# Two-layer hybrid decoder trunk on one core: where Softplus is finished, and which engines do the last LayerNorm of the second token tile

## The chip, the cores and the metric

The kernel runs on one core of a Trainium2 chip. The core has a matrix engine (TensorE, PE in the profile, with its weight loads shown as PEld), a vector engine (VectorE, DVE), an activation engine (ScalarE, ACT), a general engine (GpSimd, POOL) and a queue engine that mostly starts DMAs (SyncE, SP). Each engine works through its own instructions in order. PE writes its products into PSUM, eight banks of 128 partitions by 512 floats; the other tiles lie in SBUF. The metric is the device time of one execution in microseconds (us); less is better.

## The reference

The input is x, 256 tokens by 2048 channels. Two layers are applied, and each ends in `x <- LayerNorm(alpha * x + mixer(x))` with alpha = 4^0.25.

- Layer 0 projects x to z, xs, B, C, dt, q, k, v and a gate. The columns xs, B and C go through a causal convolution with four taps and a SiLU. `dt = softplus(dt + dt_bias)` gives the step of a state-space scan (Mamba-2 SSD, one chunk of 256 positions), beside a causal attention with 16 heads. Both results are joined and projected back.
- Layer 1 is a diagonal complex state-space mixer (S5) between an input and an output projection, with a GLU.

```
dt = jax.nn.softplus(dt.astype(f32) + dt_bias.astype(f32))
a = -jnp.exp(a_log.astype(f32))
y = ssd_chunked_scan(xh * dt[..., None], dt * a, bm, cm)
...
y = (xf - mu) * lax.rsqrt(var + LN_EPS) * g.astype(jnp.float32) + b.astype(jnp.float32)
```

All matrix products are to be near float32 in precision.

## The kernel before

**Products.** Every large weight matrix is cut into units of 128 partitions by 1024 floats, 432 in all, in the order of use. For each unit `split_to` (L217) issues a load on SP (`raw`), an ACT copy that rounds it to the fast matmul type (`wh`, L239), and a DVE subtraction that leaves the remainder (`wl`, L244). A product is the sum of three terms (high by high, high by low, low by high). `raw`, `wh` and `wl` have four buffers each, and splits are issued three units ahead of the matmuls. The matmuls of the products stand at L288 (tokens on the partitions), L310, and L343 with L344 (channels on the partitions, `product_wide`). A product alternates between two pairs of PSUM banks. The last product keeps the split tiles of all its eight units, in the pool `tp2` (L1424).

**Small work between units.** Everything else is a job: a Python function that issues a few instructions. After each unit `pump` (L260) issues some jobs of the queue `jobs`, spread so that the queue is empty at the product's end, and some of the slower queue `back`. `run` (L254) asks that a job's instructions come behind the splits of the unit two ahead. The framework then orders each engine's instructions, near this program order.

**Softplus.** `dt_mm` (L491) multiplies x by the 32 dt columns. `dt_jobs` (L508) makes five jobs on 32 partitions by 256 tokens: `soft1` (ACT and DVE: exp and a reciprocal), `soft2` and `soft3` (GpSimd, L528 to L539: a polynomial of 19 instructions), `soft4` (L541: one step that ends Softplus, L545; a scan over positions, L550; the cumulated decay as high and low parts, L551 and L552) and `turn` (L554: four small PE transposes, L559 and L560, and two ACT copies into `dts` and `cums`). `dts`, `cums` and `cumhl` are read by the head jobs of the scan, which begin in a later product.

**The xs products.** The loop at L819 runs four `product_wide` products, j = 0 to 3, for 512 xs columns each. `xs_jobs` (L803) queues, after product j, the four convolution taps of j and their SiLU (L578, L583), the transposes of the columns j - 1 that were held back, and more by j: for j = 0 the four C·B products of `cb_job` (L596) and then `soft4` and `turn`; for j = 1 `trig_job` (L616), which also loads a table on SP. These jobs are issued during product j + 1. `soft1` to `soft3` are queued ahead, so they are issued during product 0.

**The end.** The last weight matrix has four products of 512 output columns; the loop at L1435 runs the first three. After each, `res1` (L1430) adds alpha times the old x into `x1` and takes the column statistics (L1433), for the token tiles t = 0 and 1. The fourth product is `product_apart` (L392): all its matmuls for tokens 0 to 127 (t = 0), then all for tokens 128 to 255 (t = 1). After each half `after1` (L1440) queues `first` (the last `res1`, the mean and variance at L1068, adding the epsilon at L1069, the root on ACT at L1070, the reciprocal at L1071, minus mean over deviation at L1444) and four pieces of columns. Piece 3 (320 columns) is one ACT instruction (L1451) and two on GpSimd (L1452, L1453); pieces 0 to 2 (576 columns each) are two DVE instructions each: subtract the mean and multiply by the gain (L1455), then multiply by the reciprocal and add the shift (L1456). A DMA per piece (L1457) stores the rows, on SP for pieces 1 and 3 and on ACT's queue for 0 and 2. The gain and shift rows are in `gb1`, loaded on POOL's queue (L1427, L1428).

Of the kernel before, what the change touches and what calls it, by code (L numbers as in the profile page):

```python
# [9 lines left out]
F32 = mybir.dt.float32  # L10
F32R = mybir.dt.float32r
AF = mybir.ActivationFunctionType
OP = mybir.AluOpType
PSUM = bass.MemoryType.PSUM
DRAM = bass.MemoryType.DRAM

P = 128
S = 256
# [5 lines left out]
HU = KT // HK  # L24
ALPHA = 4.0 ** 0.25
NKEEP = 6
NFIRST = 4
WARM0 = 8
WARM1 = 14
# [2 lines left out]
EPS = 1e-5  # L32
# [137 lines left out]
def trunk(tc, io, out):  # L170
    nc = tc.nc
    V, A, G, T = nc.vector, nc.scalar, nc.gpsimd, nc.tensor
    count = [0]

    def nm(s):
        count[0] += 1
        return f"{s}_{count[0]}"

    with ExitStack() as top:
# [10 lines left out]
        def C(name):  # L190
            lo, hi = CONST[name]
            return ct[:, lo:hi]
# [5 lines left out]
        ident = C("ident")  # L198

        def aux():  # L200
            return auxp.tile([P, 512], F32, tag="aux", name=nm("aux"))

        def big(tag, shape, dt=F32):
            return slot.tile(shape, dt, tag=tag, name=nm(tag))
# [43 lines left out]
        jobs = deque()  # L248
# [21 lines left out]
        def drain():  # L270
            while jobs:
                run(jobs.popleft())
# [6 lines left out]
        def banks():  # L279
            turnno[0] += 1  # L280
            return [main.tile([P, 512], F32, tag=f"m{turnno[0] % 2}{o}", name=nm("main")) for o in range(2)]
# [110 lines left out]
        def product_apart(hl, nu, nk, after, mid=None):  # L392
            ps = banks()
            cap = unit[0] + nu + NFIRST - 1
            for u in range(nu - nk):
# [26 lines left out]
        def transpose4(dst, srcs):  # L422
            for i, s in enumerate(srcs):
                end = T.transpose(dst[:, i * P : i * P + P], s, ident)  # L424
            return end
# [17 lines left out]
        mr1 = cst.tile([P, 2, 4], F32, name="mr1")  # L443
        st0 = cst.tile([P, 2, 4, 6], F32, name="st0")
        st1 = cst.tile([P, 2, 4, 6], F32, name="st1")
# [4 lines left out]
        with ExitStack() as l0:  # L450
# [3 lines left out]
            def a4(shape, dt=F32):  # L454
                return wk.tile(shape, dt, tag="a4", bufs=6, name=nm("a4"))
# [113 lines left out]
            def conv_jobs(ps, ft, dst):  # L569
                acc = a4([P, 4, S])  # L570

                def tap(f):
                    def go():
                        src = ps[:, f, :] if dst is not bT and dst is not cT else ps[f // 2][:, (f % 2) * S : (f % 2) * S + S]
                        A.activation(acc[:, f, :], src, AF.Identity, bias=cb[:, ft + f : ft + f + 1], scale=cw[:, ft + f, 3:4])
                        for k in (2, 1, 0):
                            sh = 3 - k
                            V.scalar_tensor_tensor(acc[:, f, sh:], src[:, : S - sh], cw[:, ft + f, k : k + 1], acc[:, f, sh:],  # L578
                                                   op0=OP.mult, op1=OP.add)
                    return go  # L580

                jobs.extend([tap(f) for f in range(4)])
                jobs.append(lambda: A.activation(dst, acc, AF.Silu))  # L583
# [6 lines left out]
            dtj = dt_jobs()  # L590
# [5 lines left out]
            def cb_job(g):  # L596
                def go():
                    px = aux()
                    T.matmul(px[:, 0:256], bT[:, g, 0:P], cT[:, g, :], start=True, stop=True)
                    T.matmul(px[:, 256:384], bT[:, g, P:S], cT[:, g, P:S], start=True, stop=True)  # L600
                    V.tensor_tensor(cbm[:, g, 0:128], px[:, 0:128], C("tril"), op=OP.mult)
                    A.activation(cbm[:, g, 128:256], px[:, 128:256], AF.Copy)
                    V.tensor_tensor(cbm[:, g, 256:384], px[:, 256:384], C("tril"), op=OP.mult)
                return go
# [198 lines left out]
            def xs_jobs(ps, j):  # L803
                xT = a4([P, 4, S])
                conv_jobs(ps, 8 + 4 * j, xT)

                def back(t):
                    def go():
                        px = aux()
                        transpose4(px, [xT[:, f, t * P : t * P + P] for f in range(4)])  # L810
                        A.activation(xs[:, t, 512 * j : 512 * j + 512], px, AF.Copy)
                    return go

                while held:
                    jobs.append(held.popleft())
                held.extend([back(0), back(1)])
                jobs.extend({0: [cb_job(g) for g in range(4)] + dtj[3:], 1: [trig_job], 2: [table_job]}.get(j, []))

            for j in range(4):  # L819
                raw = sz[:, 4 * j : 4 * j + 4, :]  # L820
# [180 lines left out]
            for g in range(4):  # L1001
                ps = product("x", xhl)
                qT = a4([P, 4, S])
                rope_jobs(ps, qT)
                ps = product("x", xhl)
                kT = a4([P, 4, S])
                rope_jobs(ps, kT)
                ps = product("x", xhl)
# [35 lines left out]
            x1 = {}  # L1044
# [9 lines left out]
            ps = product("x", mixhl, 2 * CU, prelude=lambda u: drain() if u == 4 else None)  # L1054
            x1[0] = big("D", [P, 2, D])
            jobs.append(lambda ps=ps: res0(a4([P, 2, 512]), ps, 0, (0, 1)))
            for j in range(1, 3):
                ps = product("x", mixhl, 2 * CU)
# [5 lines left out]
        def lnrow(i):  # L1064
            return io["lnr"][i : i + 1, :].to_broadcast([P, D])
# [7 lines left out]
        with ExitStack() as lt:  # L1073
            tp = lt.enter_context(tc.tile_pool(name="tp", bufs=1))
            keep[0], keep[1] = tp, range(unit[0] + 2 * CU - NKEEP, unit[0] + 2 * CU)
            rows = [tp.tile([P, D], F32, name=f"row{i}") for i in range(2)]
# [52 lines left out]

            product_apart(tailhl, 2 * CU, NKEEP, after0, mid)  # L1130
            drain()
            x1 = x1n
# [4 lines left out]
            def first_product():  # L1137
                ps = banks()
                base = unit[0]
                split_to(base + NFIRST - 1)  # L1140

                end = {}

                def mm(u, t):
                    for j in range(UK):
                        end["i"] = xmm(ps, t, ready[base + u], j, x1hl(u * UK + j), u == 0 and j == 0, u == CU - 1 and j == UK - 1)
# [11 lines left out]
                scaled(1, 4, 4)  # L1158
                for u in range(NFIRST - 1):
                    mm(u, 0)  # L1160
                turn(1, 0)
                with tc.issue_after(end["t"].ins):
                    mm(NFIRST - 1, 0)
                scaled(1, 8, 4)
# [12 lines left out]
                turn(0, 12)  # L1177
                for u in range(NFIRST, CU):
                    if u == 5:
# [16 lines left out]
        with ExitStack() as l1:  # L1196
# [169 lines left out]
            for j in range(8):  # L1366
# [10 lines left out]
                ps = product("x", x1hl) if j else first1  # L1377
# [40 lines left out]
            for j in range(2, 8):  # L1418
                ps = product("x", y5hl)
# [3 lines left out]
        with ExitStack() as l2:  # L1423
            tp = l2.enter_context(tc.tile_pool(name="tp2", bufs=1))  # L1424
            keep[0], keep[1] = tp, range(unit[0] + 2 * CU, unit[0] + 3 * CU)
            gb1 = big("A", [P, 4, D])
            nc.gpsimd.dma_start(gb1[:, 0, :], lnrow(2))  # L1427
            nc.gpsimd.dma_start(gb1[:, 1, :], lnrow(3))  # L1428

            def res1(ps, j, t):  # L1430
                dst = x1[:, t, 512 * j : 512 * j + 512]
                V.scalar_tensor_tensor(dst, dst, ALPHA, ps[t], op0=OP.mult, op1=OP.add)
                V.bn_stats(st1[:, t, j, :], dst)  # L1433

            for j in range(3):  # L1435
                ps = product("x", y2hl, prelude=lambda u: split_to(unit[0] + 3 + u) if j == 2 else None) if j else first2
                for t in range(2):
                    jobs.append(lambda ps=ps, j=j, t=t: res1(ps, j, t))

            def after1(ps, t):  # L1440
                def first():
                    res1(ps, 3, t)
                    norm_stats(st1, mr1, t)()
                    V.scalar_tensor_tensor(mr1[:, t, 3:4], mr1[:, t, 0:1], -1.0, mr1[:, t, 2:3], op0=OP.mult, op1=OP.mult)  # L1444

                def piece(i):
                    def go():
                        sl = slice(576 * i, min(576 * i + 576, D))
                        xv = x1[:, t, sl]
                        if i == 3:  # L1450
                            A.activation(xv, xv, AF.Identity, bias=mr1[:, t, 3:4], scale=mr1[:, t, 2:3])  # L1451
                            G.tensor_tensor(xv, xv, gb1[:, 0, sl], op=OP.mult)  # L1452
                            G.tensor_tensor(xv, xv, gb1[:, 1, sl], op=OP.add)  # L1453
                        else:
                            V.scalar_tensor_tensor(xv, xv, mr1[:, t, 0:1], gb1[:, 0, sl], op0=OP.subtract, op1=OP.mult)  # L1455
                            V.scalar_tensor_tensor(xv, xv, mr1[:, t, 2:3], gb1[:, 1, sl], op0=OP.mult, op1=OP.add)  # L1456
                        (nc.sync if i % 2 else nc.scalar).dma_start(out[t * P : t * P + P, sl], xv)  # L1457
                    return go

                jobs.append(first)  # L1460
                jobs.extend([piece(i) for i in (3, 0, 1, 2)])

            product_apart(y2hl, CU, CU, after1)
            drain()

# [16 lines left out]
```

## Time and profile before

| | |
|---|---|
| median of 3 runs | 1337.47 us (1337.36 to 1339.19) |
| the profiled execution's own time | 1336.96 us |
| span of its instructions | 1335.2 us |
| instructions | 21514 |
| PE, PEld busy | 1318.7 us (99%), 1110.2 us (83%) |
| DVE, ACT, POOL busy | 960.1 us (72%), 692.6 us (52%), 343.4 us (26%) |
| granted PE clock, mean | 0.996 |

Times in the profile count from the start of the span. "L288" is line 288 of the kernel before. A row of a timeline has the start, the length, the engine, the line, the operation, the tiles written and read, and the count of merged instructions; what stands in brackets is how long the engine had been idle and what ended that. A matmul's own length is longer than its pace, since the next one starts before it ends; pace is read from start to start. A plain float32 matmul shows as two instructions. A view by stretches gives, for each engine, busy time and in brackets the count of instructions, then the granted PE clock as a share of full speed, the DMA engines' busy share and the GB/s. In the view of DMA issues, the last number is the time from the issue to the landing.

### The profile page before, as it was taken

To read this page: it belongs to the slowest core of one execution; us is meant where nothing else is said; L and a number is where in the kernel's file an instruction comes from. 1 tells how busy PE (TensorE), PEld (TensorE's weight loads), DVE (VectorE), ACT (ScalarE), POOL (GpSimd) and SP (SyncE) were. 2 spreads that over 40 slices of the span, in tenths; PEclk is the share of its full clock that TensorE was granted. 3 is DMA by queue.
4 is the path that set the end of the run, shared out by engine and by line. 5 is a ranking of instruction groups with operands and counts; after the bars stand their busy time and mean duration, and the time that the engine had idled before them with its cause. 6 is when DMAs were issued, how large, how long until landed. Compare 5 with 4: busy or idle time off the path is not lost.

```text
span 1335.2 us, 21514 instructions
## 1 busy us (share of the span) xinstructions
PE 1318.7 (99%) x8070; PEld 1110.2 (83%) x8070; DVE 960.1 (72%) x1614; ACT 692.6 (52%) x946; POOL 343.4 (26%) x648
## 2 busy tenths in 40 slices
PE   9999999999999999999999999999999999999996
PEld 8988888877888888888888888888888888888885
DVE  6776977776686777687797766858989845555556
ACT  5566667865654554554564435444345544444441
POOL 0042000121026625334787400013454100000001
PEclk9999999999999999999999999999999999999999
DMA  8544555444556656656767778388889665555762
GB/s 321 176 176 160 187 177 172 157 158 154 178 179 224 204 204 222 213 182 206 236 192 243 251 229 319 129 327 237 300 291 332 214 217 186 187 192 187 254 216 80
DMA packets 80872, 282.72 MB, mean 212 GB/s; under 512 B 9856, under 2 KB 12544, under 8 KB 80256
## 3 DMA queue, kind: packets, MB, share of 16 engines
q1 hardware_dynamic: 68256, 239.27, 53.4%
q0 software_dynamic: 7328, 30.42, 6.8%
q10 hardware_dynamic: 5184, 11.67, 2.4%
q8 instruction: 63, 1.03, 0.3%
q14 instruction: 41, 0.34, 0.1%
HBM read 260.34 MB, written 20.97 MB: 211 GB/s over the span
## 4 chain that ended last, share of the span: by engine, by line
PE 95%; POOL 2%; DMA 2%; DVE 1%; ACT 0%; issue 0%; SPq 0%; POOLq 0%; ACTq 0%; DVEq 0%
PE main L288 60%; PE main L343 15%; PE main L344 8%; PE main L310 3%; PE aux L424 2%; DMA raw<-in_wi 1%; PE aux L867 1%; PE aux L775 1%; PE enc L1275 1%; PE dec L1320 1%; PE aux L956 1%; PE aux L988 1%; POOL ew L528 0%; PE dec L1316 0%; DMA ud<-ut 0%; PE aux L785 0%
## 5 line engine op out<-in xcount | busy, mean ns | idle before, releaser
L244 DVE TENSOR_TENSOR wl<-raw,wh 128x1024 fp32r<-128x1024 f32 x430 | 532.7, 1241 | 308.8 <-ACT wh L239 305.3
L239 ACT ACTIVATE wh<-raw 128x1024 fp32r<-128x1024 f32 x430 | 455.0, 1060 | 507.5 <-PE main L288 308.9
L288 PE MATMUL main<-wh,A 128*128 128x512 f32 x1536 | 489.9, 394 | 0.0
L288 PEld LDWEIGHTS main<-wh,A 128*128 128x128 f32 x1536 | 287.8, 188 | 59.1 <-issue 0.3
L288 PE MATMUL main<-wl,A 128*128 128x512 f32 x768 | 300.7, 392 | 0.0
L343 PE MATMUL main<-A,wh 128*128 128x512 f32 x768 | 272.9, 399 | 0.0
L288 PE MATMUL main<-wh,C 128*128 128x512 f32 x832 | 262.0, 392 | 0.3 <-ACT C L1103 0.3
L344 PE MATMUL main<-A,wl 128*128 128x256 f32 x768 | 215.3, 280 | 0.0
L288 PEld LDWEIGHTS main<-wh,C 128*128 128x128 f32 x832 | 155.6, 188 | 33.5 <-ACT C L1103 1.0
L343 PEld LDWEIGHTS main<-A,wh 128*128 128x128 f32 x768 | 144.8, 188 | 33.5
L288 PEld LDWEIGHTS main<-wl,A 128*128 128x128 f32 x768 | 144.3, 188 | 29.3 <-issue 0.5
L288 PE MATMUL main<-wl,C 128*128 128x512 f32 x416 | 162.3, 390 | 0.0
L344 PEld LDWEIGHTS main<-A,wl 128*128 128x128 f32 x768 | 145.3, 189 | 0.3
L701 POOL TENSOR_TENSOR c<-c 128x8 f32<-128x8 f32 (+2 forms) x192 | 99.8, 538 | 23.6 <-DMA wb<-c 16.0
L288 PEld LDWEIGHTS main<-wl,C 128*128 128x128 f32 x416 | 78.1, 188 | 16.1
L343 PE MATMUL main<-C,wh 128*128 128x512 f32 x192 | 68.4, 400 | 0.7 <-DVE ut L355 0.7
L876 POOL TENSOR_TENSOR ssq<-ssq,c 128x256 f32<-128x256 f32 x16 | 18.3, 1147 | 172.3 <-ACT c L874 171.8
L929 POOL TENSOR_TENSOR b<-b 128x128 f32<-128x128 f32 x16 | 11.4, 710 | 194.4 <-DVE b L928 151.6
L344 PE MATMUL main<-C,wl 128*128 128x256 f32 x192 | 53.3, 282 | 0.0
L703 POOL TENSOR_TENSOR c<-c,c 128x4 f32<-128x4 f32 (+2 forms) x96 | 48.2, 502 | 7.4
L704 POOL TENSOR_TENSOR c<-c,c 128x4 f32<-128x4 f32 (+2 forms) x96 | 45.4, 473 | 0.0
L310 PE MATMUL main<-A,wh 128*128 128x256 f32 x256 | 43.5, 284 | 1.2 <-ACT wh L231 1.2
(285 smaller groups left out, 1376.6 us busy)
## 6 DMA issues: line engine op xcount, KB each, us to landing
raw<-in_wi SPq DMA_DIRECT2D x270, 512.0 KB, 3.5
raw<-in_wo SPq DMA_DIRECT2D x96, 512.0 KB, 4.2
raw<-in_wglu SPq DMA_DIRECT2D x64, 512.0 KB, 3.4
wt<-wb POOLq DMA_DIRECT2D x16, 896.0 KB, 8.8
wb<-ob ACTq DMA_DIRECT2D x16, 512.0 KB, 5.3
bc<-in_s5bc SPq DMA_DIRECT2D x16, 256.0 KB, 3.7
wb<-c POOLq DMA_DIRECT2D x16, 256.0 KB, 3.2
wb<-om ACTq DMA_DIRECT2D x16, 128.0 KB, 3.5
```

What stands on the lines that cost most here:

```text
L239: high = A.activation(wh, raw, AF.Copy)
L244: splits[n] = (loaded[-1], high, V.tensor_tensor(wl, raw, wh.bitcast(F32), op=OP.subtract))
L288: end = T.matmul(ps[o], l[:, k, sl], r[:, j, :], start=start and i == 0, stop=stop and i == 2)
L310: T.matmul(pv[o // 2][:, o % 2, :], l[:, j, sl], r[:, k, :], start=first and i == 0 and o % 2 == 0, stop=end and i == 2 and o % 2 == 1, sk ...
L343: T.matmul(ps[o], wh[:, j, sl], xx[:, k, :, :].rearrange("p a n -> p (a n)"), start=first, stop=False, skip_group_check=True)
L344: T.matmul(ps[o][:, S : 2 * S], wl[:, j, sl], xh[:, k, :], start=False, stop=end, skip_group_check=True)
L424: end = T.transpose(dst[:, i * P : i * P + P], s, ident)
L701: G.tensor_tensor(p[:, :, :, 0:m], cs[:, :, :, 1 : m + 1], cs[:, i, :, n : n + 1].unsqueeze(1).to_broadcast([P, 2, 4, m]), op=OP.mult)
L703: G.tensor_tensor(cs[:, 0, :, n + 1 : n + 1 + m], p0[:, 0, :, 0:m], p1[:, 1, :, 0:m], op=OP.subtract)
L704: G.tensor_tensor(cs[:, 1, :, n + 1 : n + 1 + m], p0[:, 1, :, 0:m], p1[:, 0, :, 0:m], op=OP.add)
L775: T.matmul(pk[at : at + 64, 64 * n + a * 16 : 64 * n + a * 16 + 16], d["ev"][:, a, 64 * i : 64 * i + 64], cv[:, a, i, :], start=True, stop ...
L876: G.tensor_tensor(ssq, ssq, jk[:, f, :], op=OP.add)
```

## The change

The first part moves two jobs. `soft4` and `turn` leave the list of j = 0, where they stood behind the four C·B products, and become the first of the list of j = 1: they are issued during product 2, behind the taps and the SiLU of the columns j = 1 and behind two held transposes, and ahead of `trig_job`.

The second part replaces `first` and the pieces for t = 1. Columns 0 to 895 of the second token tile are multiplied by the gain ahead of time, in a job that is queued behind the pieces of t = 0. After the last matmul, `last` is issued:

- PE multiplies those columns by the identity into two PSUM banks (448 columns each); a later matmul with two rows (mean and deviation, by minus the gain and the shift) adds to them, so that a bank holds x·g - mean·g + deviation·b.
- The mean and the deviation are put in a 128 by 2 tile `pair`, which PE transposes and ACT copies to be the two rows `rowp`.
- ACT multiplies each bank by the reciprocal of the deviation into `x1`.
- DVE does the other 1152 columns, 576 by 576: both instructions of the first piece, and only then (pinned by `issue_after`) those of the second. GpSimd has no part in t = 1.
- Three of the four stores are on SP, one (the second 448 columns) on ACT's queue.

The rows for the two-row matmul are a new tile `gbr`, loaded on SP at the stage's start; ACT changes the sign of its first row. Three PSUM banks are taken. The pieces of t = 0 are as before.

```diff
+NEND = 448
-                jobs.extend({0: [cb_job(g) for g in range(4)] + dtj[3:], 1: [trig_job], 2: [table_job]}.get(j, []))
+                jobs.extend({0: [cb_job(g) for g in range(4)], 1: dtj[3:] + [trig_job], 2: [table_job]}.get(j, []))
...
+            endp = l2.enter_context(tc.tile_pool(name="endp", bufs=1, space=PSUM))
+            sums = [endp.tile([P, 512], F32, name=f"sum{i}") for i in range(2)]
+            flip = endp.tile([2, P], F32, name="flip")
+            gbr = tp.tile([2, 2 * NEND], F32, name="gbr")
+            pair = tp.tile([P, 2], F32, name="pair")
+            rowp = tp.tile([2, P], F32, name="rowp")
+            nc.sync.dma_start(gbr, io["lnr"][2:4, 0 : 2 * NEND])
+            A.activation(gbr[0:1, :], gbr[0:1, :], AF.Copy, scale=-1.0)
...
+            def last(ps):
+                mr, xv = mr1[:, 1], x1[:, 1]
+                for i in range(2):
+                    T.matmul(sums[i][:, 0:NEND], ident, xv[:, NEND * i : NEND * i + NEND], start=True, stop=False)
+                res1(ps, 3, 1)
+                V.bn_aggr(pair, st1[:, 1, :, :].rearrange("p a b -> p (a b)"))
+                V.tensor_scalar(pair[:, 1:2], pair[:, 1:2], EPS, None, op0=OP.add)
+                A.activation(pair[:, 1:2], pair[:, 1:2], AF.Sqrt)
+                T.transpose(flip, pair, ident)
+                A.activation(rowp, flip, AF.Copy)
+                for i in range(2):
+                    T.matmul(sums[i][:, 0:NEND], rowp, gbr[:, NEND * i : NEND * i + NEND], start=False, stop=True)
+                cut = [slice(2 * NEND + 576 * i, 2 * NEND + 576 * i + 576) for i in range(2)]
+                V.scalar_tensor_tensor(xv[:, cut[0]], xv[:, cut[0]], pair[:, 0:1], gb1[:, 0, cut[0]], op0=OP.subtract, op1=OP.mult)
+                V.reciprocal(mr[:, 2:3], pair[:, 1:2])
+                done = V.scalar_tensor_tensor(xv[:, cut[0]], xv[:, cut[0]], mr[:, 2:3], gb1[:, 1, cut[0]], op0=OP.mult, op1=OP.add)
+                nc.sync.dma_start(out[P:S, cut[0]], xv[:, cut[0]])
+                with tc.issue_after(done.ins):
+                    V.scalar_tensor_tensor(xv[:, cut[1]], xv[:, cut[1]], pair[:, 0:1], gb1[:, 0, cut[1]], op0=OP.subtract, op1=OP.mult)
+                V.scalar_tensor_tensor(xv[:, cut[1]], xv[:, cut[1]], mr[:, 2:3], gb1[:, 1, cut[1]], op0=OP.mult, op1=OP.add)
+                for i in range(2):
+                    sl = slice(NEND * i, NEND * i + NEND)
+                    A.activation(xv[:, sl], sums[i][:, 0:NEND], AF.Copy, scale=mr[:, 2:3])
+                    (nc.scalar if i else nc.sync).dma_start(out[P:S, sl], xv[:, sl])
+                nc.sync.dma_start(out[P:S, cut[1]], xv[:, cut[1]])
+
             def after1(ps, t):
+                if t:
+                    jobs.append(lambda: last(ps))
+                    return
                 def first():
...
                 jobs.extend([piece(i) for i in (3, 0, 1, 2)])
+                jobs.append(lambda: V.tensor_tensor(x1[:, 1, 0 : 2 * NEND], x1[:, 1, 0 : 2 * NEND], gb1[:, 0, 0 : 2 * NEND], op=OP.mult))
```

## The prediction

> **What bounds the kernel now.** First the page, its busy times and the chain that ended last:
>
> ```profile
> PE 1318.7 (99%) x8070; PEld 1110.2 (83%) x8070; DVE 960.1 (72%) x1614; ACT 692.6 (52%) x946; POOL 343.4 (26%) x648
> PE 95%; POOL 2%; DMA 2%; DVE 1%; ACT 0%; issue 0%; SPq 0%; POOLq 0%; ACTq 0%; DVEq 0%
> ```
>
> PE sets the time, so an edit counts only where PE idles, where its clock falls, or behind its last matmul. In the view of PE's own waits the longest is in the code that is moved:
>
> ```profile
> PE aux L559 <- DVE ew L545: 2.1, 1, 2.1
> ```
>
> The timelines around it, POOL and DVE first, then PE:
>
> ```profile
> 83.43 6.61 POOL L528 TENSOR_TENSOR ew<-dw 32x256 f32<-32x256 f32 x1 [81.88 <-ACT a L575]
> ...
> 108.57 0.71 POOL L539 TENSOR_TENSOR ew<-ew 32x256 f32<-32x256 f32 x1
> 109.31 0.41 DVE L545 SCALAR_TENSOR_TENSOR ew<-ew,dw 32x256 f32<-32x256 f32 x1 [5.00 <-POOL ew L539]
> ```
> ```profile
> 106.93 0.40 PE L343 MATMUL main<-A,wh 128*128 128x512 f32 x1
> 107.17 0.28 PE L344 MATMUL main<-A,wl 128*128 128x256 f32 x1
> 107.29 0.39 PE L343 MATMUL main<-A,wh 128*128 128x512 f32 x1
> 109.78 0.24 PE L559 MATMUL aux<-consts,ew 32*128 32x32 f32 x1 [2.10 <-DVE ew L545]
> ```
>
> GpSimd's polynomial lasts from 83.4 to 109.3. DVE stands 5.00 us with L545 at the head of its queue, and PE 2.10 us with the first transpose of `turn` at the head of its own, with the matmuls of product 2 behind it. Stretches of 1 us show a second price:
>
> ```profile
> 110.00:111.00 1.00, 1.00 (x6) 0.86 (x6) 0.96 (x4) 0.00 (x0) 0.00 (x0) 0.81 0.00 0
> 111.00:112.00 1.00, 1.00 (x6) 0.56 (x4) 1.00 (x2) 0.93 (x2) 0.00 (x0) 0.50 0.00 0
> 112.00:113.00 1.00, 1.00 (x5) 0.84 (x5) 1.00 (x4) 1.00 (x4) 0.00 (x0) 0.50 0.08 16
> 113.00:114.00 1.00, 1.00 (x5) 0.90 (x4) 0.94 (x3) 0.13 (x2) 0.00 (x0) 0.50 0.83 188
> 114.00:115.00 1.00, 1.00 (x7) 0.87 (x7) 1.00 (x3) 0.63 (x1) 0.00 (x0) 0.99 0.80 311
> ```
>
> The third number from the right is the granted clock. Behind the stall PE is busy again, but at half speed until 114.
>
> The other place is the tail: DVE's timeline there, then the last matmul, the root on ACT, the last of GpSimd and the last store:
>
> ```profile
> 1324.22 0.69 DVE L1432 SCALAR_TENSOR_TENSOR D<-D,main 128x512 f32<-128x512 f32 x1 [3.72 <-PE main L288]
> ...
> 1326.04 2.27 DVE L1455 SCALAR_TENSOR_TENSOR D<-D,mr,A 128x576 f32<-128x576 f32 x3
> 1328.22 0.16 DVE L1071 RECIPROCAL mr<-mr 128x1 f32<-128x1 f32 x1
> ...
> 1328.49 2.87 DVE L1456 SCALAR_TENSOR_TENSOR D<-D,mr,A 128x576 f32<-128x576 f32 x3
> ```
> ```profile
> 1323.80 0.39 PE L288 MATMUL main<-wh,C 128*128 128x512 f32 x1
> 1326.16 0.20 ACT L1070 ACTIVATE mr<-mr 128x1 f32<-128x1 f32 x1 [7.77 <-DVE mr L1069]
> 1330.83 1.25 POOL L1453 TENSOR_TENSOR D<-D,A 128x320 f32<-128x320 f32 x1
> 1332.11 0.33 SPq L1457 DMA_DIRECT2D out_x<-D  x1
> ```
>
> PE ends at 1324.19. DVE does three subtractions before the reciprocal, though ACT's root is there at 1326.36, so ACT's piece and then GpSimd's start late; the last store is issued at 1332.11, and the span (1335.2) ends 3.1 us behind.
>
> **Part one, `soft4` and `turn`.** Moved are eight instructions of `soft4` (six on DVE, two on ACT, one with a table load), four PE transposes and two ACT copies; no DMA, and SP's and POOL's queues keep their order. What leaves PE's path is the 2.10 us and the slow clock, 0.19 + 3 × 0.50 + 0.01 = 1.70 us: 3.8 us.
>
> In the new place ten jobs (four taps, SiLU, two held transposes, `soft4`, `turn`, `trig_job`) go behind product 2's units as 2, 2, 2, 1, 1, 1, 1, so `turn` comes behind the sixth. A unit is eight pairs of L343 and L344, and a pair takes 0.36 us (106.93 to 107.29), so `turn` is issued some 6 × 2.9 = 17 us into a product that starts at about 107: near 124, while GpSimd is done at 109.3. What is late next is the end of Softplus, whose first reader on PE is far off:
>
> ```profile
> 113.30 0.41 DVE L552 TENSOR_TENSOR cumhl<-dw,cumhl 32x256 fp32r<-32x256 f32 x1
> L837 PE MATMUL aux<-cumhl,sel x32: 277/279/387, 187.2 to 297.7; 128*128 128x256 f32 x32
> ```
>
> From L545 to the end of L552 it is 4.4 us, so a start near 121 still ends 60 us ahead of L837. The covers are thus DVE's and ACT's idle time in product 2; without them the cost is PE idling behind a transpose again, at most those 4.4 us and a slow clock. Bounds of part one: a gain of 3.8 us, or none if the stall is only moved. I take 3.8, since every input is there early.
>
> The Trainium skill's "TensorE: Matmul & The Clock Gate", section "Part 1: The HAM clock gate", says that the clock halves after an idle window of about 3.4 us and comes back after a busy one as long. Here the time at half speed, 2 × 1.70 = 3.4 us, agrees; that 2.10 us of idling brought it on does not, unless a partly idle window is enough. By the rule the slow stretch would not be the stall's doing, and the sum would hold 2.1 us for this part instead of 3.8.
>
> **Part two, the tail.** The pace of its new pieces, by the nearest rows (a timeline of the C·B products, and groups by line and form, whose last number before the bar is the mean in ns):
>
> ```profile
> 87.38 0.59 PE L599 MATMUL aux<-a,a 128*128 128x256 f32 x2
> 87.81 0.38 PE L600 MATMUL aux<-a,a 128*128 128x128 f32 x2
> L288 PEld LDWEIGHTS main<-wh,A 128*128 128x128 f32 x1536 | 287.8, 188 | 59.1 <-issue 0.3
> L424 PE MATMUL turn<-consts,p 128*128 128x128 f32 x40 | 6.0, 272 | 0.0
> L602 ACT ACTIVATE C<-aux 128x128 f32<-128x128 f32 x4 | 0.9, 257 | 0.0
> L811 ACT ACTIVATE C<-aux 128x512 f32<-128x512 f32 x8 | 4.7, 582 | 0.0
> L575 ACT ACTIVATE a<-main,params 128x256 f32<-128x256 f32 x8 | 4.3, 555 | 1.9 <-DVE a L578 1.9
> ```
>
> - PE: a plain float32 matmul of 256 columns takes 0.43 us to the next start (87.38 to 87.81), so 448 take 0.75, and 0.17 more until the last result is out (0.38 less half of 0.43). The two by the identity end at about 1325.9, under DVE's statistics; the cover is 0.5 us wide.
> - ACT: 128 and 512 plain PSUM columns cost 0.257 and 0.582, so 256 cost 0.365; with scale and bias by pointer they cost 0.555, 0.19 more. A bank of 448 with its scale: 0.53 + 0.19 = 0.72.
> - The chain: root 1326.36; transpose 0.27; ACT copy 0.26; weights 0.19; first bank 0.75 + 0.17; ACT 0.72; ACT on the second bank 0.72, which is ready by then; five handovers of 0.03 (1324.19 to 1324.22). The second store is issued at 1326.36 + 3.08 + 0.15 = 1329.6.
> - DVE: four times 0.76 (2.27 / 3; the 2.87 of L1456 falls under GpSimd, which now has no part) and the reciprocal's 0.16 from 1326.04: 1329.2, store at 1329.3.
>
> So the last store is issued 2.5 us earlier. It has 224 KB, and 736 KB go out within 0.8 us; by the landing times of the stores now I take 0.3 off:
>
> ```profile
> DMA to landing us min/median/max: 2.0/2.2/2.4
> ```
>
> Part two gives 2.2 us. Bounds: 2.9 if the pointer costs nothing and landing stays at 2.0; a loss of 1.1 if PE runs the transpose and the two banks at half speed (1.8 more) and the identity products stand between matmuls of the last product (1.5 more). I take the chain's value, because its rows are of the same engines and kinds. The multiplication by the gain (896 columns, under twice the 0.69 us of 512) is free: DVE idles 3.72 us before 1324.22, and the columns are ready a product earlier. Without that cover it costs 1.3. DVE's wait for ACT's root holds up only the two pieces behind it; it is over at 1326.4, before the first subtraction ends.
>
> The new load of `gbr` is small and goes on SP at the start of the stage; the sign change makes ACT wait for it, with weight splits queued behind:
>
> ```profile
> 1242.14 1.06 ACT L239 ACTIVATE wh<-raw 128x1024 fp32r<-128x1024 f32 x1 [1.66 <-PE main L288]
> 1244.86 1.06 ACT L239 ACTIVATE wh<-raw 128x1024 fp32r<-128x1024 f32 x1 [1.66 <-PE main L288]
> 1248.59 1.06 ACT L239 ACTIVATE wh<-raw 128x1024 fp32r<-128x1024 f32 x1 [2.67 <-DMA raw<-in_wo]
> A<-in_lnr POOLq DMA_DIRECT2D x2, 1024.0 KB, 7.6
> ```
>
> A unit is 2.72 us here (1242.14 to 1244.86). A split starts when PE frees the buffer four units back, so PE needs it 3 × 2.72 = 8.2 us later, less some 2.2 for both halves of the split: 6 us of slack. At 1248.59 ACT is 1.0 us late and PE does not wait. A load of a few us costs nothing.
>
> **The sum.** Against the profiled execution: 1336.96 - 3.8 - 2.2 = 1331.0. The median of the runs is 0.5 higher (1337.47), so 1331.5. A difference of 0.2%, 2.7 us, is about what a measurement of this kernel can tell from none: below 1334.8 is faster, above 1340.1 slower.
>
> **Rivals.**
>
> - The tail's PE work is dear: half speed after the last matmul, or the identity products ahead of it. For it: PE's clock has fallen once after 2.1 us of idling. Against: PE's new idling is from 1325.9 to 1326.4 and about 0.3 us more, and the last product's matmuls were issued before and are all ready. 1331.5 + 1.5 to 1.8 = 1333.2.
> - The slow stretch stays, because something else than the stall brings it on: 1331.5 + 1.7 = 1333.2. For it: it sets in near 110.6 (0.81 over that us), when PE has been busy again for 0.8 us. Against: that is 3 us behind the start of PE's longest wait, and the clock is full again 3.4 us later. This is the result that the Trainium skill's rule on the clock gate, above, would give.
> - The stall is only moved, the change not doing what it says: `turn` is again at PE's head before DVE has done L545 and L550. For it: the chain is 4.4 us long and DVE is over 90% busy from 110 to 114. Against: no wait for GpSimd is left. Part one gives nothing: 1335.3, no difference.
> - Slower: ACT is held at the sign change by `gbr`, whose memory or place on SP's queue makes it late. The point from which it decides: 5 us beyond ACT's usual start PE idles; with 1.7 us for the clock it takes 12 us to reach 1340.2, and 13 us give 1331.5 + 8 + 1.7 = 1341. For it: a load in this stage took 7.6 us. Against: that had 1 MB, and ACT's wait for a load there was 2.67.
>
> **Chances.** Forecast 0.62 (its own range 1330.2 to 1332.5), dear tail 0.16, slow stretch stays 0.08, stall moved 0.08, held ACT 0.06. Faster is the sum of the first three, 0.86; same 0.08; slower 0.06. The range reaches from both parts at their best, 1330.8, less 0.9 for the spread of the runs, to the moved stall: 1329.9 to 1335.3.
>
> **What would show it.** Part one is right if no wait of PE for L545 is left, the clock stays at 1.00 from 104 to 120, and `turn` stands about 15 us later; wrong if L559 or L560 heads PE's waits. Part two is right if the reciprocal follows the first subtraction and the last store is issued 5.4 us behind PE's last product matmul (now 7.9); wrong if the identity matmuls stand before that matmul, or the two-row matmuls take more than 0.75 us each. A PE wait near 1250 for `wh` or `wl` would show the held ACT. The forecast is wrong as a whole if PE idles in a new place: the framework sorts each engine's instructions anew.

## The result, and the profile after

| | before | after |
|---|---|---|
| median of 20 runs each, side by side | 1337.18 us (1335.79 to 1343.17) | 1332.84 us (1332.00 to 1337.10) |
| ratio, 95% interval | | 0.9964 [0.9954, 0.9973] |
| profiled execution, its span | 1336.96, 1335.2 us | 1332.58, 1330.8 us |
| granted PE clock, mean | 0.996 | 0.999 |

The change saves 4.3 us by the medians and 4.4 us by the profiled executions; 6.0 were forecast, and the time lies 1.3 us above the forecast of 1331.5, inside the whole range (1329.9 to 1335.3) and 0.3 us above the forecast's own (1330.2 to 1332.5). From line 27 to 1426 a line of after has the number of before plus one (L545 is L546, L559 is L560); the tail is numbered anew.

First PE's own waits, after:

```profile
PE aux L434 <- DVE idle L429: 1.0, 1, 1.0
PE flip L1457 <- ACT pair L1456: 0.7, 1, 0.7
PE main L344 <- DVE ut L356: 0.5, 1, 0.5
PE main L311 <- ACT wh L232: 0.4, 2, 0.2
PE sum L1460 <- ACT rowp L1458: 0.4, 1, 0.4
PE main L289 <- ACT C L1104: 0.3, 1, 0.3
```

The wait for L545 (now L546) is gone and no wait of that size has come in. The two new rows, `flip` and `sum`, are the tail's. The stretches of 1 us that ran at half speed before:

```profile
110.00:111.00 1.00, 1.00 (x8) 0.86 (x7) 1.00 (x2) 1.00 (x1) 0.94 (x1) 1.00 0.01 4
111.00:112.00 1.00, 1.00 (x8) 0.86 (x7) 1.00 (x4) 0.05 (x1) 0.92 (x2) 1.00 0.00 0
112.00:113.00 1.00, 1.00 (x9) 0.91 (x8) 1.00 (x2) 0.19 (x1) 0.57 (x1) 1.00 0.88 233
```

The clock (third number from the right) is 1.00, and PE does eight or nine instructions per us where it did five or six. `turn` on PE, and the end of Softplus and of its split on DVE:

```profile
123.15 0.24 PE L560 MATMUL aux<-consts,ew 32*128 32x32 f32 x1
...
124.36 0.22 PE L561 MATMUL aux<-consts,dw 32*128 32x32 f32 x1
```
```profile
119.25 0.40 DVE L546 SCALAR_TENSOR_TENSOR ew<-ew,dw 32x256 f32<-32x256 f32 x1
...
122.75 0.42 DVE L553 TENSOR_TENSOR cumhl<-dw,cumhl 32x256 fp32r<-32x256 f32 x1
```

The transposes start 13.4 us later than before (109.78), and their inputs are there: no number stands in brackets behind them. The tail, all engines in order of time:

```profile
1321.37 0.39 PE L289 MATMUL main<-wh,C 128*128 128x512 f32 x1
...
1321.60 1.66 PE L1452 MATMUL sum<-D,consts 128*128 128x448 f32 x4
...
1323.62 0.81 DVE L1462 SCALAR_TENSOR_TENSOR D<-D,pair,A 128x576 f32<-128x576 f32 x1
1323.74 0.20 ACT L1456 ACTIVATE pair<-pair 128x1 f32<-128x1 f32 x1 [8.08 <-DVE pair L1455]
...
1323.99 0.27 PE L1457 MATMUL flip<-consts,pair 128*2 128x128 f32 x1 [0.73 <-ACT pair L1456]
1324.30 0.27 ACT L1458 ACTIVATE rowp<-flip 2x128 f32<-2x128 f32 x1 [0.36 <-PE flip L1457]
1324.35 0.16 DVE L1463 RECIPROCAL mr<-pair 128x1 f32<-128x1 f32 x1
...
1324.62 1.77 PE L1460 MATMUL sum<-gbr,rowp 2*128 2x448 f32 x4 [0.35 <-ACT rowp L1458]
...
1325.67 1.39 ACT L1471 ACTIVATE D<-sum,mr 128x448 f32<-128x448 f32 x2 [1.10 <-PE sum L1460]
1326.12 0.82 DVE L1468 SCALAR_TENSOR_TENSOR D<-D,mr,A 128x576 f32<-128x576 f32 x1
...
1326.97 0.33 SPq L1473 DMA_DIRECT2D out_x<-D  x1
1327.09 0.34 ACTq L1472 DMA_DIRECT2D out_x<-D  x1
```

The last product ends on PE at 1321.37 + 0.39 = 1321.76, and the last store is issued at 1327.09, 5.33 us behind (before: 7.92). The reciprocal stands behind one subtraction, not three. The span ends 3.7 us behind that store (before: 3.1), which the landing time of that one store explains, in the view of DMA issues:

```profile
out_x<-D ACTq DMA_DIRECT2D x1, 224.0 KB, 2.7
```

**Where the 4.4 us come from.** The same matmul can be found in both profiles by its number among those of its line. Its start before minus its start after is PE's lead, so its growth over a stretch is what after gains there:

```
near, us (before)    60     118    140    190    260 to 860   1000 to 1295   1313   last (1323.80 - 1321.37)
lead, us           -0.05   3.96   3.27   2.68      2.60          3.06        2.74   2.43
```

PE is 3.96 us ahead at 118, of which the four transposes, which come later now, take back some 0.45. By 190 another 0.9 are lost. Near 900 and 1000 there come 0.46 in two steps, in layer 1, where nothing was changed; a second profile of the kernel before (e11, below) gains 1.0 us there on the first profile of the same kernel. In the last product 0.6 go again. Behind the last product matmul 11.4 us became 9.43: 1.97 gained. 2.43 + 1.97 = 4.4.

The loss up to 190 and that in the last product were in no term of the forecast. Both show as a slower pace of matmuls that wait for nothing. First the product with channels on the partitions: two rows of before, two of after, each pair with 126 steps from start to start between them (63 pairs of L343 and L344) and no other matmul:

```profile
149.69 0.28 PE L344 MATMUL main<-A,wl 128*128 128x256 f32 x1
...
171.53 0.28 PE L344 MATMUL main<-A,wl 128*128 128x256 f32 x1
```
```profile
146.52 0.28 PE L345 MATMUL main<-A,wl 128*128 128x256 f32 x1
...
168.78 0.28 PE L345 MATMUL main<-A,wl 128*128 128x256 f32 x1
```

21.84 us before, 22.26 after: 0.3467 and 0.3533 us a pair. Then the last product, 94 steps from the start of its second matmul (the two rows below) to the start of its last (at 1323.80 before, in the prediction; at 1321.37 after, above):

```profile
1302.49 0.39 PE L288 MATMUL main<-wl,C 128*128 128x512 f32 x1
```
```profile
1299.44 0.39 PE L289 MATMUL main<-wl,C 128*128 128x512 f32 x1
```

21.31 us before, 21.93 after: 0.2267 and 0.2333 us a matmul. The two products ahead of it run at 0.2267 in both.

### The profile page after: what moved, and what is told of

It is laid out like the page before. It is cut to its first block, busy times and chain, and to the rows that moved or that the text cites. A ratio compares the mean times of both kernels' runs of the same rounds, so it can differ in the third digit from the quotient of the medians.

```text
span 1330.8 us, 21538 instructions
## 1 busy us (share of the span) xinstructions
PE 1323.0 (99%) x8079; PEld 1112.8 (84%) x8079; DVE 961.5 (72%) x1612; ACT 691.7 (52%) x947; POOL 339.8 (26%) x646
## 4 chain that ended last, share of the span: by engine, by line
PE 98%; DMA 1%; ACT 0%; DVE 0%; SPq 0%; issue 0%; ACTq 0%
PE main L289 61%; PE main L344 17%; PE main L345 8%; PE main L311 3%; PE aux L425 2%; PE aux L868 1%; PE aux L776 1%; PE enc L1276 1%; PE dec L1321 1%; PE aux L957 1%; PE aux L989 1%; DMA ud<-ut 0%; PE dec L1317 0%; DMA raw<-in_wi 0%; PE aux L786 0%; PE aux L838 0%
## 5 line engine op out<-in xcount | busy, mean ns | idle before, releaser
L344 PE MATMUL main<-A,wh 128*128 128x512 f32 x768 | 273.1, 399 | 0.0
L344 PEld LDWEIGHTS main<-A,wh 128*128 128x128 f32 x768 | 144.4, 188 | 33.4
L344 PE MATMUL main<-C,wh 128*128 128x512 f32 x192 | 68.4, 400 | 0.5 <-DVE ut L356 0.5
L930 POOL TENSOR_TENSOR b<-b 128x128 f32<-128x128 f32 x16 | 11.4, 711 | 196.0 <-DVE b L929 153.3
L704 POOL TENSOR_TENSOR c<-c,c 128x4 f32<-128x4 f32 (+2 forms) x96 | 44.0, 459 | 7.4
L705 POOL TENSOR_TENSOR c<-c,c 128x4 f32<-128x4 f32 (+2 forms) x96 | 45.4, 473 | 0.0
```

What stands on the lines that cost most here:

```text
L344: T.matmul(ps[o], wh[:, j, sl], xx[:, k, :, :].rearrange("p a n -> p (a n)"), start=first, stop=False, skip_group_check=True)
L704: G.tensor_tensor(cs[:, 0, :, n + 1 : n + 1 + m], p0[:, 0, :, 0:m], p1[:, 1, :, 0:m], op=OP.subtract)
L705: G.tensor_tensor(cs[:, 1, :, n + 1 : n + 1 + m], p0[:, 1, :, 0:m], p1[:, 0, :, 0:m], op=OP.add)
```

## The experiments

Two questions: is each part worth what the prediction said when it stands alone, and what makes the matmuls slower. In the first four the suspicion was that the kept split tiles of the last product (`tp2`), which the new small tiles push to other addresses, set its pace. The addresses below are bytes per partition in the compiled program. Of the two operands of the last product, `C` holds the activations and is loaded into PE as its 128 by 128 weights; it stands at 55776 in all but two kernels (e6 and e7). The kept split tiles stream past it as the 512 moving columns; they begin at 154080 before and at 158208 after.

**e1, the first part alone.** Before with

```diff
-                jobs.extend({0: [cb_job(g) for g in range(4)] + dtj[3:], 1: [trig_job], 2: [table_job]}.get(j, []))
+                jobs.extend({0: [cb_job(g) for g in range(4)], 1: dtj[3:] + [trig_job], 2: [table_job]}.get(j, []))
```

> Only the two Softplus jobs are moved; the tail is that of before. Theory: the 2.1 us stall of PE and the 1.7 us of slow clock go, so PE is 3.6 to 3.8 us ahead at 120 us of the span, the clock stays at 1.00 from 104 to 120, the last product's matmuls keep a pace of 0.227 us, and the time is 2.5 to 3.8 us below that of before. After the stall of before, matmul pairs of the channel products ran at 0.347 us from 122 to 190 against 0.353 ahead of it; the theory that the stall itself brought that quicker stretch expects 0.353 there in this run and about 1 us lost again by 190 (2.6 us ahead in the end). Rival, that the quicker stretch is chance: 0.347 as often as 0.353, and up to 3.6 us ahead in the end.

Measured 1333.7 us, ratio 0.9970 [0.9959, 0.9980]: 3.6 us less than before beside it. The last product runs at 0.2267. The lead gained from 60 to 118 is 4.0 us, as in after, and the 126 steps of the slower pace behind it take 22.26 us, as in after, so that loss does not come from the tail. The profiled execution was the longest of its runs (1336.94); in PE's waits it has two in layer 1 that the profiles of before and after lack, 3.0 us together:

```profile
PE dec L1316 <- ACT ys L1326: 1.9, 1, 1.9
PE enc L1275 <- DMA wt<-wb: 1.1, 1, 1.1
```

Such waits come and go between executions of one program: e8, which is after unchanged, has 0.6 us of PE's wait for `ys` that after has not. The runs of one kernel lie up to 5 us apart or more, so parts below 1 us are read here from rows and not from medians.

**e2, the second part alone.** After with the line of e1 turned back.

> Only the second part; soft4 and turn stay in the list of j = 0. Theory: the stall of 2.1 us and the slow clock are back; the span behind the last product matmul is 9.0 us instead of 11.0; the kept weight tiles of the last product lie at an address that leaves 0 on division by 64 instead of 32, and its 96 matmuls run at 0.233 us instead of 0.227, which costs 0.6 us. Time 1.4 us below before. If the slower pace came from something in the moved jobs, the pace here is 0.227 and the time 2.0 us below before.

Measured 1336.63 us, ratio 0.9992 [0.9982, 1.0003]: 0.7 us less, not told apart from none. Behind the last product matmul (1326.10) stand 9.6 us to the span's end, against 11.4 before, so the tail alone gains its 1.8. The last product at 0.2333 takes back 0.6, and the profile has 1.5 us of such a wait in layer 1 besides. With `turn` in its old place the stall is back, and so is the slow clock:

```profile
PE aux L560 <- DVE ew L546: 2.3, 1, 2.3
PE dec L1317 <- ACT ys L1327: 1.5, 1, 1.5
```
```profile
110.00:111.00 1.00, 1.00 (x6) 0.75 (x6) 0.96 (x3) 0.05 (x1) 0.00 (x0) 0.98 0.00 0
111.00:112.00 1.00, 1.00 (x6) 0.78 (x6) 1.00 (x2) 1.00 (x2) 0.00 (x0) 0.50 0.00 0
```

**e3 and e4, the kept tiles moved.** After with the kept tiles 32 bytes higher (at 158240), and before with them 32 bytes higher (154112), by an unused tile:

```diff
-            pair = tp.tile([P, 2], F32, name="pair")
+            pair = tp.tile([P, 16], F32, name="pair")[:, 0:2]
```
```diff
             gb1 = big("A", [P, 4, D])
+            shim = tp.tile([P, 8], F32, name="shim")
```

> The changed kernel with the tile pair made 64 instead of 8 bytes wide, so that the kept weight tiles are 32 bytes further on (32 left on division by 64, as in the kernel before). Nothing else differs. Theory of the placement: the last product's pace is 0.227 us again and PE ends 0.6 us earlier than in the changed kernel: 5.0 us below before. Rival (the slower pace has another cause, such as the state of the clock or the load of DMA and ACT in the last product): 0.233 us stays and the time is that of the changed kernel, 4.4 us below before.

> The kernel before with an unused tile of 32 bytes ahead of the kept weight tiles in their pool, so that these leave 0 on division by 64. No instruction is added or moved. Theory of the placement: the last product runs at 0.233 us and the time is 0.6 us above before, all of it in the last 22 us of PE. Rival: pace 0.227 and no difference.

e3: 1331.74 us, ratio 0.9963 [0.9949, 0.9977]; its last product, again 94 steps, takes 21.52 us, 0.2289 a matmul, between the two paces:

```profile
1298.65 0.40 PE L289 MATMUL main<-wl,C 128*128 128x512 f32 x1
...
1320.17 0.39 PE L289 MATMUL main<-wh,C 128*128 128x512 f32 x1
```

e4: 1338.67 us, ratio 1.0005 [0.9990, 1.0019]. No instruction was changed, and the last product runs at 0.2333. Its rows, again 94 steps, 21.93 us:

```profile
1303.50 0.39 PE L288 MATMUL main<-wl,C 128*128 128x512 f32 x1
...
1325.43 0.40 PE L288 MATMUL main<-wh,C 128*128 128x512 f32 x1
```

So the place of the tiles matters, but e3 did not give the full pace back: the rule was still missing. The clock of e4 stayed full behind the stall, which no expectation had foreseen:

```profile
PE aux L559 <- DVE ew L545: 2.3, 1, 2.3
```
```profile
111.00:112.00 1.00, 1.00 (x8) 0.88 (x9) 1.00 (x2) 1.00 (x2) 0.00 (x0) 1.00 0.08 16
112.00:113.00 1.00, 1.00 (x7) 0.90 (x6) 0.97 (x4) 1.00 (x5) 0.00 (x0) 1.00 0.13 41
```

**e5 to e8, alignment to 128 bytes.** After with `pair` as [P, 32] (e5: kept tiles at 158304, modulo 128 the same as before); the same with an unused tile of 32 (e6) or 64 bytes (e7) ahead of all others, so that every operand of the last product is moved; after unchanged (e8).

```diff
+        shim = cst.tile([P, 8], F32, name="shim")
```

> The changed kernel with the tile pair 128 bytes wide: the kept weight tiles of the last product then leave 96 on division by 128, as in the kernel before (0 in the changed kernel, 32 in e3). Theory of the placement, by residues of 128: pace of the last product 0.2267 us, PE ends 0.6 us earlier than in the changed kernel and 0.2 us earlier than in e3; time 0.6 us below the changed kernel run beside it (e8). Rival, residues of 64 alone: as e3, 0.2289.

> The kernel of e5 with 32 unused bytes ahead of all tiles: products' operands, stationary and moving, all leave 0 on division by 128 (96 in e5). No instruction differs. If the place of the moving operand by itself sets the pace, every product with weights as the moving operand (3552 matmuls) runs at 0.2333 instead of 0.2267 us and the time is about 23 us above e5. If the distance between the two operands sets it, the pace stays 0.2267 and the time is that of e5.

> As e6 with 64 unused bytes: all operands leave 32 on division by 128. If the place of the moving operand by itself sets the pace: 0.2289 us, about 8 us above e5. If the distance between the two operands does: 0.2267 and the time of e5.

> The changed kernel once more, beside e5 on the same chip. Every theory: 1332.4 to 1333.2 us, last product at 0.2333 us, clock 1.00 from 104 to 120. What it decides is the stretch from 122 to 172 us: in the one profile of before a pair of L343 and L344 took 0.347 us there, in five others 0.353. If that is chance of the execution, 0.353 or 0.347 may come here; if the changed program fixes it, 0.353.

e5 1332.36 (ratio 0.9967 [0.9951, 0.9983]), e6 1332.43 (0.9958 [0.9944, 0.9973]), e7 1333.11 (0.9959 [0.9944, 0.9975]), e8 1332.91 (0.9967 [0.9953, 0.9982]). The last product ran at 0.2333 in all four: alignment to 64 or 128 bytes is not the rule, against the expectations of e5 to e7, and e8 shows the pace of after again. Nor is it the place of the moving tile alone: in e6 and e7 the moving tiles of the earlier products had moved too, and the 23 and 8 us that this would have cost did not come. One thing still set e5 to e7 apart from before, the distance between the two operands: 158304 - 55776 leaves 128 modulo 256, in e6 and e7 too, where both had moved.

**e9 and e10, distance a multiple of 256.** After with the kept tiles 224 bytes higher (158432) and 4064 bytes higher (162272):

```diff
-            pair = tp.tile([P, 2], F32, name="pair")
+            pair = tp.tile([P, 58], F32, name="pair")[:, 0:2]
```

(1018 instead of 58 in e10.)

> After with a longer pair tile, so that the kept split tiles of the last product start 224 bytes higher. Counted from the start of the last product's weights (C) modulo 4096, the kept tiles then stand at 256 bytes; they stood at 0 in the two kernels with the quick last product (0.2267 us a matmul), at 32 or 128 in those with 0.2333, and at 64 in the one with 0.229. Theory that the distance of the two operands modulo 256 bytes sets the pace: 0.2267, a last product 96 x 0.0067 = 0.6 us shorter, near 1332.3. Rival, a longer modulus (512 to 4096): not 0.2267 here, but 0.2267 in the next kernel, and 1332.9. Rival, placement has no part: 0.2333 in both.

> After with a pair tile so long that the kept split tiles start 4064 bytes higher, 8192 above where before has them: distance 0 modulo 4096 from the weights C. By either placement theory 0.2267 us a matmul in the last product and 0.6 us off the time of after: near 1332.3. If placement has no part: 0.2333 and 1332.9.

Measured 1331.88 us (ratio 0.9958 [0.9943, 0.9973]) and 1332.12 us (0.9955 [0.9938, 0.9972]). The last product of e9:

```profile
1299.33 0.39 PE L289 MATMUL main<-wl,C 128*128 128x512 f32 x1
...
1320.64 0.40 PE L289 MATMUL main<-wh,C 128*128 128x512 f32 x1
```

21.31 us, 0.2267 a matmul, and the same in e10: a distance of 256 does as well as one of 0, and e5 to e7 had shown that one of 128 does not; so the period is 256 bytes, as far as these distances tell. The 0.6 us are back. By their medians both stand below after, but the intervals overlap, so as whole kernels they are not told apart from it.

**e11 and e12, before again, and before with the kept tiles 256 bytes higher** (the tile of e4 with [P, 64]).

> Before unchanged, for a second profile. If the quick stretch from 122 to 190 (a pair of L343 and L344 in 0.347 us instead of 0.353) belongs to the program, it is there again; if it was of that one execution, 0.353 throughout. The last product at 0.2267 by the placement theory. PE waits for L545 2.1 to 2.3 us at about 107.5 to 109.8; the clock falls for 3.413 us behind it if the wait lies in one of the windows of 3.413 us in which the clock changes, and stays at 1.00 if a boundary splits it.

> Before with an unused tile of 256 bytes per partition ahead of the kept split tiles, which then stand at 256 bytes from the weights C modulo 4096 (e4 had 32 bytes there). Placement theory with a period of 256 bytes: the last product stays at 0.2267 us a matmul and the time is that of before, 1337; a theory by which any move of the kept tiles makes it slow: 0.2333 and 0.6 us more. The quick stretch from 122 to 190 (0.347 us for a pair of L343 and L344): 0.347 if it goes with the order and the addresses of before, as in both profiles of before; 0.353 would say, as e2 and e4 did, that these do not settle it. The clock behind the wait for L545 falls for 3.413 us, or not, by where the wait lies.

e11: one run, 1335.19 us. e12: 1337.5 us, ratio 1.000 [0.9981, 1.0019], the last product at 0.2267, as the distance asks. Over all profiles the pace goes by the distance modulo 256: 0 gives 0.2267 (before twice, e1, e9, e10, e12), 64 gives 0.2289 (e3), 32 and 128 give 0.2333 (after twice, e2, e4; e5, e6, e7). It is the distance and not the address itself: e6 runs its third product of the same loop at 0.2267 with tiles whose address is 0 modulo 256, as in after's last product, but with `C` at 0 too.

The quick stretch from 122 to 190 is there again in e11 and is not in e12. From start to start over the same 126 steps, first e11, then e12:

```profile
148.83 0.28 PE L344 MATMUL main<-A,wl 128*128 128x256 f32 x1
...
170.67 0.28 PE L344 MATMUL main<-A,wl 128*128 128x256 f32 x1
```
```profile
148.53 0.28 PE L344 MATMUL main<-A,wl 128*128 128x256 f32 x1
...
170.79 0.28 PE L344 MATMUL main<-A,wl 128*128 128x256 f32 x1
```

21.84 and 22.26 us. e2, e4 and e12 have the instructions, the order and the addresses of before up to that place, and the stall, and run at 0.353. So neither the order, nor the addresses, nor the stall settles this pace. Nor does the slow clock, which e2 has as well. None of the nine profiles with the moved jobs has the quick stretch, and two of the five without have it; that is too few to say that the change takes it away, and the cause stays open.

## Why the prediction was right, and where it was off

**The stall and the slow clock: right, in place and size.** PE waits for L546 no more, the clock stays full, and `turn` stands at 123 to 124 (worked out: near 124), 13 us later and not 15. The chain behind the polynomial, from L546's start to the end of L553, takes 123.17 - 119.25 = 3.9 us (4.4 before) and ends 64 us ahead of 187.2, where L837 read it before. The lead of 3.96 less 0.45 is 3.5, near the 3.8 of the sum, and e1 alone measures 3.6 by its median.

**That the stall brought on the slow clock: right for that execution, but a matter of phase.** Five profiles have the stall (before, e11, e2, e4, e12); three have the slow clock behind it, and no profile without the stall has it there. The record of the granted clock beside the stalls, with the moments at which the clock could change (multiples of 3.413 us from where it first became full):

```
                 PE idle from..to    possible changes    clock halves at
before           107.68..109.78      107.20, 110.61      110.61 for 3.413
before again     106.80..108.91      107.61, 111.02      111.02 for 3.413
e2               107.33..109.67      107.56, 110.97      110.97 for 3.413
e4               107.14..109.48      108.57, 111.98      stays full
e12              107.38..109.72      109.18, 112.59      stays full
```

The clock fell where such a moment came 0.8 to 2.1 us behind the stall's end, and not where the next one came 2.5 or 2.9 us behind it. The expectation of e11, that the clock stays full if such a moment lies within the stall, did not hold: 107.61 lies within the stall of e11 and 107.56 within that of e2, and there the clock fell. The Trainium skill's "TensorE: Matmul & The Clock Gate", section "Part 1: The HAM clock gate", has a free-running window of 3413 ns, which these numbers bear out, and an idle window as the condition, which they do not: 2.10 us of idling sufficed. So the rival made from that rule, that the slow stretch stays, fell: without the stall it is gone. But the 1.7 us of the sum are not a fixed price of this stall; in two of five profiles they were not there to be saved.

**The tail: right within 0.2 us.** Predicted 5.4 us from PE's last product matmul to the last store, measured 5.33. By terms: the two-row matmuls and the wait for the first result 1325.67 - 1324.62 = 1.05 (0.92 predicted), ACT's two banks 1.39 (1.44), the whole chain from the root's end to the last store 1327.09 - 1323.94 = 3.15 (3.23); DVE's pieces took 0.81 or 0.82 each, not 0.76, and still end ahead of ACT's. The two two-row matmuls took 1.77 us where the two by the identity took 1.66, so they are some 0.05 us each above the 0.75 that the prediction had named as a sign of being wrong; that is the 0.1 us in the first term, and no more. What was too small is the term for the stores: they cost 0.6 us more behind the last issue, not 0.3, since the last one lands 2.7 us behind its issue. Hence 2.0 instead of 2.2. The dear tail fell here: the identity matmuls stand behind the last product matmul, end at 1323.26, 0.7 us ahead of the transpose, and the clock is full until 1327.84. It can come, though, at a smaller price than the 1.8 us of its bound: in e3 the clock fell at 1324.84, within the two-row matmuls,

```profile
1323.42 1.99 PE L1460 MATMUL sum<-gbr,rowp 2*128 2x448 f32 x4 [0.35 <-ACT rowp L1458]
...
1325.45 0.63 ACT L1471 ACTIVATE D<-sum,mr 128x448 f32<-128x448 f32 x1 [0.34 <-PE sum L1460]
```

which took 1.99 us for 1.77, and the last store came 5.55 us behind the product (1326.11 - 1320.56), 0.2 later.

**The held ACT fell.** ACT came to the sign change without having to wait for `gbr`:

```profile
1247.81 1.07 ACT L240 ACTIVATE wh<-raw 128x1024 fp32r<-128x1024 f32 x1
1248.77 0.93 ACT L1435 ACTIVATE gbr<-gbr 1x896 f32<-1x896 f32 x1
1250.49 1.06 ACT L240 ACTIVATE wh<-raw 128x1024 fp32r<-128x1024 f32 x1 [0.80 <-ACT gbr L1435]
1253.21 1.06 ACT L240 ACTIVATE wh<-raw 128x1024 fp32r<-128x1024 f32 x1 [1.66 <-PE main L289]
```

It held up no split either: the next one starts 2.72 us ahead of its follower, the pace of a unit, and ACT idled 0.80 us before it. No wait of PE shows there.

**The time alone would not have told.** 1332.84 is nearer to the 1333.2 of two rivals, the dear tail and the slow stretch that stays, than to 1331.5. The rows rule both out for this execution: the identity matmuls stand behind the last product and the clock is full from 104 to 120 and to 1327.84. What made the time longer is in the next paragraph.

**The step that was off: that nothing else on PE would change.** The sum had terms for the edited instructions and none for matmuls left as they are, whose pace it took as unchanged. The change's new tiles (3584 + 32 + 512 = 4128 bytes ahead of the kept tiles) put the operands of the last product 32 bytes off a multiple of 256, and 96 matmuls took 0.0067 us more each, 0.6 us; e4, e9, e10 and e12 show this. And before, as profiled, had a quick stretch from 122 to 190 that after does not have, 0.9 us; that the change causes this isn't shown, as said above. The account of the profiled executions: 3.8 became 3.5 at once and 2.6 by 190; 0.46 came in layer 1 by chance of the execution; 0.6 went by placement; the tail gave 2.0. 2.6 + 0.46 - 0.6 + 1.97 = 4.4.

## What to carry to other kernels

A stall at the head of PE's queue can be removed by issuing the waiting instruction later, with the producer left as it is; look first for how late its result is read next. A tail that waits on one engine can be shared out to engines that are idle there, if each new operation's price is taken from a row of its own kind. And adding a small tile moves all that is allocated behind it: where PE is the bound, compare the start-to-start pace of untouched matmuls as well as the waits, and keep the two operands of a product a multiple of 256 bytes apart (measured here on matmuls with 512 moving columns, at distances that leave 0, 32, 64 and 128).

## What the hardware showed that was not expected

- The pace of a matmul with 512 moving columns depends on the distance modulo 256 bytes between its moving tile and its weights: 0.2267 us at 0, 0.2289 at 64, 0.2333 at 32 and 128. The Trainium skill's "TensorE: Matmul & The Clock Gate", section "Part 2: What happens when you issue a matmul", says that loading weights takes no read bandwidth from the running matmul. Here the relative place of the two tiles costs up to 3%, and by what mechanism isn't shown.
- The product with L343 and L344 has two paces too, 0.3467 and 0.3533 us a pair, the same 0.0067 apart, each kept for 20 us and more, and not settled by order and addresses.
- The clock fell after 2.10, 2.11 and 2.34 us of idling and twice stayed full after 2.34: what differs is where the stall ends in a grid of 3.413 us, at most 2.11 us ahead of its next moment or at least 2.50. Idle time alone doesn't give the rule: in the tail of e3 it fell behind 0.72 and 0.35 us of idling, with a small transpose between them. What the clock counts stays open.
- An ACT instruction on one partition with 896 columns takes 0.93 us, nearly as long as the 1.06 of 128 partitions with 1024.
